# First-stage loads in one fixed order, and two blocks' sums of squares moved to GpSimd, in a hybrid Fourier/RWKV layer

## The chip, the cores and the metric

The kernel runs on one core of a Trainium2 chip. The metric is the device time in microseconds (us). Three runs of the kernel before took 1665.74, 1667.07 and 1669.72 us; the median is 1667.07. The profile comes from one more execution, whose own time is 1670.74 us and whose span, from the first to the last instruction, is 1668.9 us. Every time in the rows below is counted from the start of that span.

The engines are called as the profile calls them: PE (matrix), PEld (its weight loads), DVE (vector), ACT (scalar), POOL (GpSimd), SP (the queue that issues nearly all DMAs).

## The reference

One transformer-like layer over 1024 latent tokens of width 1024 and 256 context tokens. Only its first lines matter here:

```
mod_x = silu(c) @ ada_w + ada_b          # six vectors of 1024: shift, scale, gate, and again
mod_c = silu(c_ctx) @ ada_w + ada_b      # the same for the context
h  = rms_norm(x,   norm1_g) * (1 + scale) + shift
hc = rms_norm(ctx, norm1_g) * (1 + scale_c) + shift_c
u  = h @ w_in ;  uc = hc @ w_in[:, 512:] # the input projection
... Fourier mixing, RWKV scans, output projection, residual,
... second norm, gated feed-forward with a 3x3 grid convolution, final norm
```

All arithmetic is in 32 bits. For a product, a matrix is split into a high and a low part (`hi`, `lo`), and three products (hi·hi, lo·hi, hi·lo) are added up.

## The kernel before

The change lies in the first stage, `stage0`, and what follows it is the same program: input projection with the RWKV preparation beside it, Fourier part, scans, output projection, feed-forward. A scheduler arranges each engine's instructions in one fixed order, guided by its own model of their times; each engine then runs its own list strictly in order, and an instruction that has to wait holds up all behind it.

What stage 0 does:

- **Modulation.** `load_ad(q)` (L270) loads a 2 MB piece `ad` of `ada_w`, 512 of its 6144 columns. Pieces 0 and 1 give the shift for channels 0 to 511 and 512 to 1023, pieces 2 and 3 the scale. `ada_rows` (L276) multiplies a piece with the conditioning vector: 32 PE instructions, each recorded as two matmuls (x64 at L283), and ACT copies the result (`br`, L286). PE turns it (L292), and DVE adds the bias into `mod` (L321). Pieces 4 to 11 belong to later stages; the generator `ada_rest`, here `rest`, loads and multiplies them a little at a time. There are two buffers for pieces.
- **Positions.** x and ctx lie transposed, channels on partitions, in three blocks: two of 512 positions and the 256 of the context (`BLOCKS`). A block is eight tiles `x`, one for each k, that is each 128 channels.
- **`norm`** (L332) squares the eight tiles on ACT (L337), with two buffers `sq`, and adds the squares up on DVE (L339) into `sqs`. PE sums over the channels (L342); ACT and DVE form the reciprocal root `rs` (L264, L267); DVE writes four diagonal tiles `dg` (L348, two buffers), and PE spreads them over all partitions (`rsb`, L349).
- **`enter`** (L352) makes the two parts of h: for each k DVE forms v = x·G·rsb (L355, three buffers), ACT the high part hTh = v + shift (L357), DVE the low part hTl (L358). G comes from the scale (L368).
- **Products** (L385) of each block with two column tiles of `w_in` (m = 12 and 13) into `plat` and `pctx`. `weights` (L254) loads a tile (`wraw`, one buffer here), ACT writes its high part `whi` (L188), POOL its low part `wlo` (L189).

The first instruction after stage 0 that counts is the first product of the next column tile (L197), on PE.

**What sets the order of the loads.** All of them are issued by SP in the order of its list. A load waits until its buffer is free. It also waits until the load eight places before it has landed, since the program has eight semaphores for them.

Of the kernel before, what the change touches and what calls it, by code (L numbers as in the profile page):

```python
# [10 lines left out]
F32 = mybir.dt.float32  # L11
F32R = mybir.dt.float32r
# [151 lines left out]
class B:  # L164
# [105 lines left out]
    def load_ad(self, q):  # L270

        ad = self.wa.tile([128, 8, 512], F32, name="ad", bufs=2)
        self.nc.sync.dma_start(ad, self.a["ada"][:, :, q * 512:(q + 1) * 512])
        return ad
# [36 lines left out]
    def stage0(self, wk, hT, first, rest):  # L311
# [12 lines left out]
        def load_x(b, n):  # L324
            xs = []
            for k in range(8):
                x = wk.tile([128, 512], F32, name="x", bufs=16)[:, :n]
                nc.sync.dma_start(x, a["xT"][:, k, b:b + n])
                xs.append(x)
            return xs  # L330

        def norm(b, n, xs):  # L332
            who = int(b == T)
            acc = wk.tile([128, 512], F32, name="sqs", bufs=2)[:, :n]
            for k, x in enumerate(xs):
                sq = wk.tile([128, 512], F32, name="sq", bufs=2)[:, :n] if k else acc
                nc.scalar.activation(sq, x, AF.Square)  # L337
                if k:
                    nc.vector.tensor_add(acc, acc, sq)  # L339
# [12 lines left out]
        def enter(b, n, xs, rsb, who):  # L352
            for k, x in enumerate(xs):
# [6 lines left out]
        ads = [self.load_ad(2), self.load_ad(3)]  # L360
        self.adab = self.load("adab")
        self.n1g = self.load("n1g")
        self.n2g = self.load("n2g")
        xs = {0: load_x(*BLOCKS[0])}
        for q in (2, 3):
            modulation(q, ads.pop(0))
            ads.append(self.load_ad(q - 2))
        nc.vector.scalar_tensor_tensor(G, mod[:, 8:16, :], 1.0, self.n1g[:, :, None].to_broadcast([128, 8, 2]),  # L368
                                       op0=OP.add, op1=OP.mult)
        ws = [self.weights(self.wp, a["wi"][m], raws=1) for m in first]  # L370
        for n in (1, 2):
            xs[n] = load_x(*BLOCKS[n])
        stats = norm(*BLOCKS[0], xs[0])
        for q in (0, 1):
            modulation(q, ads[q])
        us = [(self.pl.tile([128, T], F32, name="plat", bufs=2), pp.tile([128, TC], F32, name="pctx", bufs=2)) for m in first]
        for n, (b, w) in enumerate(BLOCKS):
            if n:
                stats = norm(b, w, xs[n])
            enter(b, w, xs[n], *stats)  # L380
            for (wh, wl), (ul, uc) in zip(ws, us):
                o = uc if b == T else ul[:, b:b + w]
                for k in range(8):
                    for i, (wt, xt) in enumerate(((wh, hi), (wh, lo), (wl, hi))):
                        nc.tensor.matmul(o, wt[:, k, :], xt[:, k, b:b + w], start=k == 0 and i == 0, stop=k == 7 and i == 2)  # L385
            next(rest)
        return [[(ul, slice(0, T)), (uc, slice(T, TT))] for ul, uc in us]


    def stage1_open(self, wk):  # L390
        nc, a = self.nc, self.a
        const = self.const
        for n in ("cw", "w0", "a0", "kk_", "ka_", "rk_", "gng", "gnb", "bones", "bk", "mask"):
            setattr(self, n, self.load(n))
# [1136 lines left out]
```

## Time and profile before

| | |
|---|---|
| median of three runs | 1667.07 us (1665.74 to 1669.72) |
| profiled execution: time, span | 1670.74 us, 1668.9 us |
| busy: PE, DVE, ACT, POOL | 1506.0, 1120.0, 703.0, 510.6 us |
| granted PE clock, mean | 0.946 of full speed |
| stage 0, by its last product on PE | ends at 91.2 us |

How to read it: a busy share is an average over stages with different limits. For a change in one stage, the engine timelines of that stage say more: each row gives the start and the length of an instruction (or of neighbours of one kind), and in square brackets how long its engine had been idle before and what ended the wait. "PEclk" is the granted PE clock: 1.00 is 2.4 GHz and 0.50 is 1.2 GHz. DMA queue rows ("SPq") give the issue of a load, not its landing.

### The profile page before, as it was taken

Reading aid. Unit: us, or ns where it says so; the run is one execution under the profiler, and the core shown is the slowest. Engines: PE = TensorE matmul, PEld = TensorE weight load, DVE = VectorE, ACT = ScalarE, POOL = GpSimd, SP = SyncE. Lnnn points to the kernel's source line nnn. Section 1 sums busy time; section 2 is a strip of 40 time slices with the busy share of each in tenths; the row PEclk is TensorE's granted clock in tenths of the full one; section 3 lists DMA queues with packets and bytes.
Section 4 is the critical chain, followed back from the end, with each engine's and each line's share of the span. In section 5 each row is a group of like instructions: output and inputs, shape, how many; then the busy total and the mean of one; then the engine's idle time right before and its main releaser. Section 6 shows DMA issues by size and latency. Waiting matters only on the chain. (4 is left out here: it accounts for less than half of the span.)

```text
span 1668.9 us, 29107 instructions
## 1 busy us (share of the span) xinstructions
PE 1506.0 (90%) x11642; PEld 1217.8 (73%) x11642; DVE 1120.0 (67%) x1599; ACT 703.0 (42%) x1193; POOL 510.6 (31%) x443
## 2 busy tenths in 40 slices
PE   4899899898877689997988999999999998999996
PEld 3687676666656577786767888888888886786785
DVE  3614756666597786844556799999999998415513
ACT  3434656666443344426575322222222223445533
POOL 0013624443332342302132222222221222454454
PEclk7899999999977888999999999999999999999998
DMA  8676857787877687746310311111111116444542
GB/s 306 219 289 204 255 181 220 231 236 224 210 210 140 182 218 197 222 142 189 120 42 14 119 51 51 51 51 49 40 51 51 51 51 214 139 129 155 174 134 90
DMA packets 219319, 246.29 MB, mean 148 GB/s; under 512 B 63638, under 2 KB 173344, under 8 KB 219184
## 3 DMA queue, kind: packets, MB, share of 16 engines
q1 hardware_dynamic: 213008, 233.92, 46.1%
q0 software_dynamic: 6176, 10.51, 2.4%
q8 instruction: 92, 1.51, 0.4%
q14 instruction: 43, 0.35, 0.1%
HBM read 177.99 MB, written 66.33 MB: 146 GB/s over the span
## 5 line engine op out<-in xcount | busy, mean ns | idle before, releaser
L189 POOL TENSOR_TENSOR wlo<-wraw,whi 128x1024 fp32r<-128x1024 f32 x105 | 255.0, 2429 | 669.0 <-ACT whi L188 612.9
L1248 DVE SCALAR_TENSOR_TENSOR conv<-u,c_fcw,conv 128x945 f32<-128x945 f32 (+2 forms) x344 | 411.5, 1219 | 37.0 <-ACT conv L1241 29.1
L188 ACT ACTIVATE whi<-wraw 128x1024 fp32r<-128x1024 f32 x123 | 129.4, 1053 | 306.4 <-issue 173.7
L197 PE MATMUL u<-h2l,whi 128*128 128x512 f32 x672 | 207.0, 389 | 0.0
L197 PE MATMUL u<-h2h,whi 128*128 128x512 f32 x672 | 206.8, 389 | 0.0
L197 PE MATMUL u<-h2h,wlo 128*128 128x512 f32 x672 | 206.8, 389 | 0.0
L189 DVE TENSOR_TENSOR al<-act,ah 128x256 fp32r<-128x256 f32 (+1 forms) x88 | 62.8, 718 | 139.2 <-ACT ah L188 139.1
L197 PEld LDWEIGHTS u<-h2l,whi 128*128 128x128 f32 x672 | 126.1, 188 | 26.3
L197 PEld LDWEIGHTS u<-h2h,wlo 128*128 128x128 f32 x672 | 126.1, 188 | 26.2
L197 PEld LDWEIGHTS u<-h2h,whi 128*128 128x128 f32 x672 | 126.1, 188 | 26.0
L1305 PE MATMUL e<-wlo,ah 128*128 128x512 f32 x264 | 103.0, 390 | 2.9 <-POOL wlo L189 2.9
L1305 PE MATMUL e<-whi,al 128*128 128x512 f32 x264 | 103.0, 390 | 0.0
L188 ACT ACTIVATE ah<-act 128x256 fp32r<-128x256 f32 (+1 forms) x88 | 45.9, 523 | 134.8 <-PE e L1305 99.3
L197 PE MATMUL plat<-hTh,whi 128*128 128x512 f32 x272 | 97.1, 439 | 0.0
L197 PE MATMUL plat<-hTl,whi 128*128 128x512 f32 x272 | 90.4, 413 | 0.0
L197 PE MATMUL plat<-hTh,wlo 128*128 128x512 f32 x272 | 88.4, 404 | 0.4 <-DVE wlo L672 0.4
L1305 PE MATMUL e<-whi,ah 128*128 128x512 f32 x264 | 67.0, 389 | 0.0
L935 POOL COPY WV<-SV 64x512 f32<-64x512 f32 x40 | 27.7, 692 | 127.9 <-PE py L1001 33.7
L856 DVE TENSOR_TENSOR arrt<-arr 128x30 f32<-128x30 f32 (+9 forms) x150 | 53.4, 356 | 15.2 <-DMA arr<-xad 11.0
L197 PEld LDWEIGHTS plat<-hTl,whi 128*128 128x128 f32 x272 | 52.0, 194 | 14.0 <-issue 2.4
L197 PEld LDWEIGHTS plat<-hTh,wlo 128*128 128x128 f32 x272 | 52.3, 194 | 12.8 <-DVE wlo L672 0.8
L563 DVE TENSOR_TENSOR_SCAN cs<-c_rst,sg 128x256 f32<-128x256 f32 x40 | 33.2, 831 | 42.0 <-ACT sg L547 36.2
(290 smaller groups left out, 3090.0 us busy)
## 6 DMA issues: line engine op xcount, KB each, us to landing
wraw<-wd SPq DMA_DIRECT2D x66, 512.0 KB
ad<-ada SPq DMA_DIRECT2D x12, 2048.0 KB
wraw<-wu SPq DMA_DIRECT2D x42, 512.0 KB
xrd<-x SPq DMA_DIRECT2D x32, 640.0 KB
xs<-xrd SPq DMA_DIRECT2D x16, 1280.0 KB
xad<-x SPq DMA_DIRECT2D x80, 192.0 KB
xs<-xad SPq DMA_DIRECT2D x18, 512.0 KB
kvb<-kvd SPq DMA_DIRECT2D x16, 512.0 KB
```

Of the source, the lines that this page charges most:

```text
L188: self.nc.scalar.activation(hi, x, AF.Copy)
L189: (lo_eng or self.nc.gpsimd).tensor_sub(lo, x, hi.bitcast(F32))
L197: mm = self.nc.tensor.matmul(ps[:, b:b + n], wt[:, k, :], xt[:, k, b:b + n], start=k == 0 and i == 0, stop=k == 7 and i == 2)
L563: nc.vector.tensor_tensor_scan(cs, self.rst, o(sg), 0.0, op0=OP.mult, op1=OP.add)
L856: nc.vector.tensor_tensor(tv, arr[:, 0:j, j:j + 1].to_broadcast(sh), arr[:, j:j + 1, j + 1:].to_broadcast(sh), op=OP.mult)
L935: nc.gpsimd.tensor_copy(wv[r, h], sv[r, h])
L1248: nc.vector.scalar_tensor_tensor(og[:, R, Cc], ug[:, Ri, Ci], self.fcw[:, m, w:w + 1], og[:, R, Cc], op0=OP.mult, op1=OP.add)
L1305: nc.tensor.matmul(t, x[:, 128 * (i - i0):128 * (i - i0) + 128], w[:, j, 512 * (b - b0):512 * (b - b0) + 512], start=k == 0 and m == 0, st ...
```

## The change

1. The loads of stage 0 are chained: each is told to stand behind the one before on SP (`self.behind(self.link)`). The sequence is pieces 2 and 3 (scale), bias and first norm vector, the first block of x, first weights (m = 12), piece 0 (shift), second weights (m = 13), piece 1, the second and third block of x, and then `n2g`, the first of the later pieces, and the constants of the next stage.
2. The tiles `x` get 24 buffers, where they had 16.
3. In the second and third block the squares are added up on GpSimd (now L354).
4. Block 0 enters in two halves. Channels 0 to 3 need only piece 0; the products of tile m = 12 over them stand on PE ahead of the rows of piece 1, and the rest follows.

The diff, whole:

```diff
--- before.py
+++ after.py
@@ -270,7 +270,7 @@
     def load_ad(self, q):
 
         ad = self.wa.tile([128, 8, 512], F32, name="ad", bufs=2)
-        self.nc.sync.dma_start(ad, self.a["ada"][:, :, q * 512:(q + 1) * 512])
+        self.ad_load = self.nc.sync.dma_start(ad, self.a["ada"][:, :, q * 512:(q + 1) * 512])
         return ad
 
     def ada_rows(self, ad):
@@ -324,10 +324,25 @@
         def load_x(b, n):
             xs = []
             for k in range(8):
-                x = wk.tile([128, 512], F32, name="x", bufs=16)[:, :n]
-                nc.sync.dma_start(x, a["xT"][:, k, b:b + n])
+                x = wk.tile([128, 512], F32, name="x", bufs=24)[:, :n]
+                with self.behind(self.link):
+                    self.link = nc.sync.dma_start(x, a["xT"][:, k, b:b + n])
                 xs.append(x)
             return xs
+
+        def load_ad(q):
+            with self.behind(self.link):
+                ad = self.load_ad(q)
+            self.link = self.ad_load
+            return ad
+
+        def load_w(m):
+            raw = self.wp.tile([128, 8, 128], F32, name="wraw", bufs=1)
+            with self.behind(self.link):
+                self.link = nc.sync.dma_start(raw, a["wi"][m])
+            hi, lo = [self.wp.tile([128, 8, 128], F32R, name=x, bufs=2) for x in ("whi", "wlo")]
+            self.split(hi, lo, raw)
+            return hi, lo
 
         def norm(b, n, xs):
             who = int(b == T)
@@ -336,7 +351,7 @@
                 sq = wk.tile([128, 512], F32, name="sq", bufs=2)[:, :n] if k else acc
                 nc.scalar.activation(sq, x, AF.Square)
                 if k:
-                    nc.vector.tensor_add(acc, acc, sq)
+                    (nc.gpsimd if b else nc.vector).tensor_add(acc, acc, sq)
             st = pp.tile([128, 512], F32, name="aux")
             for i in range(n // 128):
                 nc.tensor.matmul(st[:, i:i + 1], acc[:, 128 * i:128 * i + 128], self.ones[:, 0:1], start=True, stop=True)
@@ -349,41 +364,59 @@
                 nc.tensor.matmul(rsb[:, 128 * i:128 * i + 128], self.ones, dg, start=True, stop=True)
             return rsb[:, :n], who
 
-        def enter(b, n, xs, rsb, who):
-            for k, x in enumerate(xs):
+        def enter(b, n, ks, rsb, who):
+            for k in ks:
+                x = xs[b][k]
                 v = wk.tile([128, 512], F32, name="v", bufs=3)[:, :n]
                 nc.vector.scalar_tensor_tensor(v, x, G[:, k, who:who + 1], rsb, op0=OP.mult, op1=OP.mult)
                 h, l = hi[:, k, b:b + n], lo[:, k, b:b + n]
                 nc.scalar.activation(h, v, AF.Identity, bias=mod[:, k, who:who + 1])
                 nc.vector.scalar_tensor_tensor(l, v, mod[:, k, who:who + 1], h.bitcast(F32), op0=OP.add, op1=OP.subtract)
 
-        ads = [self.load_ad(2), self.load_ad(3)]
+        def products(b, n, tiles, ks):
+            for m in tiles:
+                (wh, wl), (ul, uc) = ws[m], us[m]
+                o = uc if b == T else ul[:, b:b + n]
+                for k in ks:
+                    for i, (wt, xt) in enumerate(((wh, hi), (wh, lo), (wl, hi))):
+                        mm = nc.tensor.matmul(o, wt[:, k, :], xt[:, k, b:b + n], start=k == 0 and i == 0, stop=k == 7 and i == 2)
+            return mm
+
+        ads = {2: self.load_ad(2), 3: self.load_ad(3)}
         self.adab = self.load("adab")
         self.n1g = self.load("n1g")
-        self.n2g = self.load("n2g")
+        self.link = self.ad_load
         xs = {0: load_x(*BLOCKS[0])}
-        for q in (2, 3):
-            modulation(q, ads.pop(0))
-            ads.append(self.load_ad(q - 2))
+        ws = []
+        for q, m in zip((2, 3), first):
+            modulation(q, ads[q])
+            ws.append(load_w(m))
+            ads[q - 2] = load_ad(q - 2)
         nc.vector.scalar_tensor_tensor(G, mod[:, 8:16, :], 1.0, self.n1g[:, :, None].to_broadcast([128, 8, 2]),
                                        op0=OP.add, op1=OP.mult)
-        ws = [self.weights(self.wp, a["wi"][m], raws=1) for m in first]
-        for n in (1, 2):
-            xs[n] = load_x(*BLOCKS[n])
+        for b, n in BLOCKS[1:]:
+            xs[b] = load_x(b, n)
+        loads = self.loaded = self.link
+        with self.behind(loads):
+            self.n2g = self.load("n2g")
+        us = [(self.pl.tile([128, T], F32, name="plat", bufs=2), pp.tile([128, TC], F32, name="pctx", bufs=2)) for m in first]
         stats = norm(*BLOCKS[0], xs[0])
-        for q in (0, 1):
-            modulation(q, ads[q])
-        us = [(self.pl.tile([128, T], F32, name="plat", bufs=2), pp.tile([128, TC], F32, name="pctx", bufs=2)) for m in first]
-        for n, (b, w) in enumerate(BLOCKS):
-            if n:
-                stats = norm(b, w, xs[n])
-            enter(b, w, xs[n], *stats)
-            for (wh, wl), (ul, uc) in zip(ws, us):
-                o = uc if b == T else ul[:, b:b + w]
-                for k in range(8):
-                    for i, (wt, xt) in enumerate(((wh, hi), (wh, lo), (wl, hi))):
-                        nc.tensor.matmul(o, wt[:, k, :], xt[:, k, b:b + w], start=k == 0 and i == 0, stop=k == 7 and i == 2)
+        modulation(0, ads[0])
+        b, n = BLOCKS[0]
+        enter(b, n, range(4), *stats)
+        mm = products(b, n, (0,), range(4))
+        with self.behind(mm):
+            modulation(1, ads[1])
+        enter(b, n, range(4, 8), *stats)
+        products(b, n, (1,), range(4))
+        products(b, n, (0, 1), range(4, 8))
+        with self.behind(loads):
             next(rest)
+        for b, n in BLOCKS[1:]:
+            enter(b, n, range(8), *norm(b, n, xs[b]))
+            products(b, n, (0, 1), range(8))
+            next(rest)
+        self.link = None
         return [[(ul, slice(0, T)), (uc, slice(T, TT))] for ul, uc in us]
 
 
@@ -391,7 +424,8 @@
         nc, a = self.nc, self.a
         const = self.const
         for n in ("cw", "w0", "a0", "kk_", "ka_", "rk_", "gng", "gnb", "bones", "bk", "mask"):
-            setattr(self, n, self.load(n))
+            with self.behind(self.loaded):
+                setattr(self, n, self.load(n))
 
         for n in ("w0", "a0"):
             t = getattr(self, n)
```

The scheduler made new lists from this. Three places are shown, with names as in the code; line numbers above 340 have moved, so that L328 became L329, L337 L352, L339 L354, L342 L357, L349 L364, L357 L373, L385 L382, and the load of first weights L342.

SP, from the first tiles of x on, before:

```order
L328 DMA x<-xT 128x512 x8
L256 DMA wraw<-wi 128x1024
L328 DMA x<-xT 128x512 x8
L183 DMA c_cw<-cw 128x36
L183 DMA c_w_789<-w 128x8
L183 DMA c_a_791<-a 128x8
L273 DMA ad<-ada 128x8x512
L183 DMA c_kk__793<-kk_ 128x4
```

and now:

```order
L329 DMA x<-xT 128x512 x8
L342 DMA wraw<-wi 128x1024
L273 DMA ad<-ada 128x8x512
L342 DMA wraw<-wi 128x1024
L273 DMA ad<-ada 128x8x512
L329 DMA x<-xT 128x512 x8
L329 DMA x<-xT 128x256 x8
L183 DMA c_n2g<-n2g 128x8
L273 DMA ad<-ada 128x8x512
L183 DMA c_cw<-cw 128x36
```

Pieces 0 and 1 and the second weights now stand ahead of the second block of x, and the constants behind everything that stage 0 needs.

ACT, from the second block's squares to the last high part of block 0, before:

```order
L337 ACTIVATE sq<-x 128x512 x6
L286 ACTIVATE br<-aux 128x128
L357 ACTIVATE hTh<-v,mod 128x512 x3
L188 ACTIVATE whi<-wraw 128x1024
L337 ACTIVATE sqs<-x 128x256
L357 ACTIVATE hTh<-v,mod 128x512
L337 ACTIVATE sq<-x 128x256 x2
L286 ACTIVATE br<-aux 128x128
L337 ACTIVATE sq<-x 128x256 x3
L357 ACTIVATE hTh<-v,mod 128x512 x3
```

and now:

```order
L286 ACTIVATE br<-aux 128x128
L373 ACTIVATE hTh<-v,mod 128x512 x3
L352 ACTIVATE sqs<-x 128x512
L373 ACTIVATE hTh<-v,mod 128x512
L352 ACTIVATE sq<-x 128x512 x4
L352 ACTIVATE sqs<-x 128x256
L352 ACTIVATE sq<-x 128x512 x2
L286 ACTIVATE br<-aux 128x128
L352 ACTIVATE sq<-x 128x512
L373 ACTIVATE hTh<-v,mod 128x512 x3
L352 ACTIVATE sq<-x 128x256 x2
L373 ACTIVATE hTh<-v,mod 128x512
```

The first `br` in each is that of piece 0, the second that of piece 1. The squares of block 1 stood ahead of the first; seven of its eight, and one of block 2, now stand between the two.

PE, around the spreading of block 1's norm (the rows of `ad` in between are those of piece 4), before:

```order
L349 MATMUL aux<-dg,ones 128x128
L283 MATMUL aux<-ad,sc_93 32x128 x7
L349 MATMUL aux<-dg,ones 128x128
L283 MATMUL aux<-ad,sc_93 32x128 x13
L349 MATMUL aux<-dg,ones 128x128
L283 MATMUL aux<-ad,sc_93 32x128 x3
```

and now:

```order
L364 MATMUL aux<-dg,ones 128x128
L283 MATMUL aux<-ad,sc_93 32x128 x5
L364 MATMUL aux<-dg,ones 128x128
L283 MATMUL aux<-ad,sc_93 32x128 x13
L364 MATMUL aux<-dg,ones 128x128
L283 MATMUL aux<-ad,sc_93 32x128 x8
L364 MATMUL aux<-dg,ones 128x128
L283 MATMUL aux<-ad,sc_93 32x128 x6
```

Before, the first of the four spreads stands a few rows further up, with nine of the rows and four products behind it; the place on PE is otherwise the same.

## Rows read from the trace of the kernel before

**Rows 1.** Busy time by stretch: PE, PEld, DVE, ACT, POOL, clock, DMA share, GB/s.
```profile
0.00:92.00 92.00, 60.76 (x551) 48.78 (x555) 46.39 (x96) 38.56 (x67) 5.55 (x8) 0.85 0.68 239
92.00:200.00 108.00, 102.19 (x924) 77.46 (x917) 47.20 (x76) 48.85 (x104) 41.63 (x41) 0.99 0.84 270
...
460.00:700.00 240.00, 191.45 (x3060) 157.41 (x3060) 190.48 (x435) 99.41 (x211) 77.29 (x108) 0.82 0.76 193
```

**Rows 2.** PE timeline: start, length, instruction, idle before and what ended it.
```profile
24.81 1.84 PE L342 MATMUL aux<-ones,sqs 128*128 128x1 f32 x8 [2.06 <-DVE sqs L339]
...
31.12 1.22 PE L349 MATMUL aux<-dg,ones 128*128 128x128 f32 x4 [0.51 <-DVE dg L348]
35.58 3.64 PE L283 MATMUL aux<-ad,sc 128*32 128x128 f32 x64 [3.23 <-DMA ad<-ada]
...
62.67 0.38 PE L349 MATMUL aux<-dg,ones 128*128 128x128 f32 x2
...
67.08 0.49 PE L349 MATMUL aux<-dg,ones 128*128 128x128 f32 x2
...
92.80 0.73 PE L197 MATMUL plat<-hTh,whi 128*128 128x512 f32 x2
```

**Rows 3.** DVE timeline.
```profile
40.05 0.17 DVE L321 TENSOR_TENSOR mod<-aux,c_adab 128x8 f32<-128x8 f32 x1 [4.00 <-PE aux L292]
...
48.44 2.04 DVE L358 SCALAR_TENSOR_TENSOR hTl<-v,mod,hTh 128x512 fp32r<-128x512 f32 x1 [3.38 <-ACT hTh L357]
...
56.69 0.16 DVE L321 TENSOR_TENSOR mod<-aux,c_adab 128x8 f32<-128x8 f32 x1
...
59.63 0.74 DVE L358 SCALAR_TENSOR_TENSOR hTl<-v,mod,hTh 128x512 fp32r<-128x512 f32 x1
...
67.60 2.07 DVE L355 SCALAR_TENSOR_TENSOR v<-x,G,aux 128x512 f32<-128x512 f32 x3 [2.10 <-PE aux L349]
```

**Rows 4.** SP's queue: issues of loads.
```profile
26.89 0.55 SPq L273 DMA_DIRECT2D ad<-ada  x1
...
35.88 0.55 SPq L273 DMA_DIRECT2D ad<-ada  x1
...
51.50 8.57 SPq L328 DMA_DIRECT2D x<-xT  x2
```

**Rows 5.** Busy time and DMA rate while loads queue up; columns as in rows 1.
```profile
10.00:20.00 10.00, 7.67 (x129) 6.62 (x129) 1.91 (x4) 2.80 (x5) 0.00 (x0) 1.00 1.05 376
```

**Rows 6.** ACT timeline.
```profile
2.44 1.28 ACT L309 ACT_TABLE_LOAD   x1 [2.44 <-DMA c_cv<-cv]
...
24.16 1.06 ACT L188 ACTIVATE whi<-wraw 128x1024 fp32r<-128x1024 f32 x1 [0.42 <-DMA wraw<-wi]
...
27.57 0.26 ACT L264 ACTIVATE rs<-aux,eps 128x4 f32<-128x4 f32 x1
...
30.11 0.63 ACT L337 ACTIVATE sq<-x 128x512 f32<-128x512 f32 x1 [0.36 <-DVE sqs L339]
...
39.27 0.28 ACT L286 ACTIVATE br<-aux 128x128 f32<-128x128 f32 x1 [6.75 <-PE aux L283]
```

**Rows 7.** POOL timeline.
```profile
47.56 2.37 POOL L189 TENSOR_TENSOR wlo<-wraw,whi 128x1024 fp32r<-128x1024 f32 x1 [19.91 <-ACT whi L188]
```

**Rows 8.** Single lines: instructions, ns shortest/median/longest, first and last start.
```profile
L1332 POOL TENSOR_TENSOR x<-x,fgb x8: 1278/1642/1752, 1439.4 to 1655.2; 128x512 f32<-128x512 f32 x8
...
L583 POOL TENSOR_TENSOR bt<-kd x16: 729/905/1178, 166.2 to 475.8; 128x256 f32<-128x256 f32 x16
...
L1248 DVE SCALAR_TENSOR_TENSOR conv<-u,c_fcw,conv x344: 1189/1205/1271, 930.7 to 1409.0; 128x945 f32<-128x945 f32 x86, 128x1008 f32<-128x1008 f32 x43, 128x960 f32<-128x960 f32 x43
...
L189 DVE TENSOR_TENSOR wol<-wor,woh x8: 685/694/1770, 586.6 to 784.7; 128x512 fp32r<-128x512 f32 x8
```

**Rows 9.** Clock in short stretches; columns as in rows 1.
```profile
48.00:50.00 2.00, 2.00 (x19) 1.43 (x12) 1.56 (x1) 1.19 (x4) 1.93 (x1) 0.50 1.07 392
...
52.00:54.00 2.00, 2.00 (x11) 1.61 (x10) 0.00 (x0) 0.00 (x0) 0.00 (x0) 1.00 1.06 389
```

## The prediction

> **What bounds the kernel now.** I read the page first, then busy time by stretch, then the timelines of the first stage engine by engine. The stretches show where the change can act at all: in the first 92 us PE is busy for 60.8 us at a mean clock of 0.85, and from 92 to 200 us for 102.2 of 108 us at 0.99 [rows 1]. So the first stage is bound by waits of PE, and the stage behind it by PE itself. The border is the first product of the next column tile, at 92.80 us [rows 2]. What comes after waits for that point through PE's list, and no load behind it has a clock of its own, so I take a shift of this point as a shift of the end, one for one.
>
> Inside the first stage three moments pace everything. The shift for channels 0 to 511 is there at 40.05, that for 512 to 1023 at 56.69, and the first v of block 1 starts at 67.60 [rows 3]. From that v to 92.80 it is 25.2 us, in which DVE and PE run through blocks 1 and 2 with almost the same list before and after. Hence the gain is the number of us by which v of block 1 comes earlier. The two shifts are late because pieces 0 and 1 are issued at 26.89 and 35.88 [rows 4], behind sixteen tiles of x and most of the constants; PE starts on piece 0 at 35.58 having waited for the load [rows 2]. The last tiles of x are issued from 51.50 on, one of them held up for 8.57 us by its buffer [rows 4].
>
> **The change part by part.** All times are on the scale of the trace.
>
> *The loads.* Queued loads move 376 GB/s [rows 5]: a 2.1 MB piece takes 5.6 us, a 0.26 MB tile 0.7, 0.52 MB of weights 1.4. The first weights had landed by 24.16 [rows 6], and piece 0 is now right behind them: landed between 27.5 and 29.7. The second weights have one raw buffer with the first, so SP stands still until POOL has made `wlo` of the first: 24.16 + 1.06 for ACT [rows 6] + 2.37 for POOL [rows 7] is 27.7. This stop is new, and all later loads queue behind it. A load into an empty queue took from 0.76 to 2.44 here (the landing is in [rows 6]), so 1.7 us. The second weights land at 27.7 + 1.7 + 1.4 = 30.8, piece 1 at 36.5, the tiles of block 1 from 37.2 to 42, those of block 2 until 45, piece 4 at about 50.5, with the constants behind it. Removing `n2g` from the head, and the 24 buffers, save nothing by themselves.
>
> *First shift.* Block 0's norm loses the squares and sums of block 1 that stood in between. Its sum on PE ends at 26.65 [rows 2]; `rs`, which came at 27.57 after two foreign squares, comes at 26.8; the diagonals follow, and the four spreads take 0.6 us each at half clock [rows 2], until 30.1. The rows of piece 0 stand behind them on PE, so the landing no longer decides: 30.1 + 3.64 for the rows [rows 2] = 33.7. Before, the shift stood 0.8 us after the rows ended (39.22 to 40.05). Now 34.6, a gain of 5.5 us.
>
> *Second shift.* PE would have the rows of piece 1 at about 42 to 43.6. But ACT's copy `br` now stands behind six more squares of block 1 and one of block 2, and each square needs one of two buffers, which POOL's adds free. So POOL's pace enters here. No 128x512 add on POOL is in the trace of before; the nearest are a 128x512 multiplication, 1.28 us alone and up to 1.75, and a 128x256 add, 0.73 to 1.18 [rows 8]. I take 1.4 and 0.95, near the lower end, because for the first five adds DVE is nearly idle. The first square of block 1 ends at 37.8, the second, behind a high part of 0.7, at 39.1; the seven adds end at 40.6, 42.0, 43.4, 44.8, 46.2, 47.6 and 49.0. The seventh square waits for the fourth add: 44.8 + 0.6 [rows 6], then `br` 0.3 [rows 6] and 0.5 to the shift: 46.3. Gain 10.4 us. With 1.28 per add it is 45.8, with 1.75 it is 47.7.
>
> *Second half of block 0, and norm of block 1.* Its four low parts hTl on DVE take 0.74 us each [rows 3]. While POOL made the second `wlo`, from 47.56 to 49.93 [rows 7], one of them that started at 48.44 took 2.04 [rows 3]: it ended 0.55 after POOL did, so it stood still beside it. DVE's convolutions, which read one operand from PSUM, never took more than 1.27 in 344 runs [rows 8], with POOL's splits of weights beside many of them. So adds on POOL and low parts on DVE take turns. The first low part waits for the seventh add (49.0); then three adds of block 2 and four low parts alternate, 4 x 0.65 + 3 x 0.95 = 5.4, until 54.4; if DVE went first throughout it would be 51.6. I take 54. The reciprocal and the first diagonal stand behind them on DVE: 0.7 us, so the first spread is at 54.8. PE's 24 products of this half keep pace: 2 us hold some ten of them at full clock and half as many at 0.50 [rows 9], and even with half clock for the first half they end by 55.5. From the first spread to v it took 62.67 to 67.60, 4.9 us, 0.9 of them for four products that now stand elsewhere, so 4.0 at full clock, or up to 7 at half. Before, PE came to this place at 1.00; now it has had a pause from about 43.6 to 46.9, and in this stage the clock was still at 0.50 at 48 to 50 [rows 9]. I put 0.5 on top: v of block 1 at 59.3 instead of 67.6.
>
> *The sum.* 67.6 - 59.3 = 8.3 us. The profiled execution would come to 1670.7 - 8.3 = 1662.4; the median of the three runs lies 3.7 below the profiled execution, so 1667.1 - 8.3 = 1658.8 us.
>
> The adds taken from DVE (14, at about 0.6 and 0.3 us) give nothing beyond this: where they stood DVE was waiting for the shifts. The constants that DVE needs beside the diagonals land at about 51, under the low parts; were that cover gone, DVE would wait 1 to 2 us. Piece 4, whose rows stand between the spreads on PE, lands 4 us before they are reached.
>
> The Trainium skill has a rule that speaks against the fourth item ("SBUF — State Buffer", section "Who interferes with whom"): a DVE instruction with two SBUF inputs and a GpSimd instruction that reads SBUF cannot run together, and the one that comes second waits for the whole of the other. By that rule hTl, with both inputs in SBUF, waits, and v and the convolutions, with one in PSUM, don't; the trace agrees, with 2.04 us against 0.74 and 1.27 at most. Without the rule the sum would be 2.4 us better, v at 56.9.
>
> **The rivals.** *POOL stays out of the way* (A). The adds take 1.28, DVE goes first, the clock stays up. Then the second shift is at 45.8, the low parts end at 51, the products at 53, and v starts at 57; with the clock up early and squares that find their tiles sooner, 54. The gain is 10.6 to 13.6, and the time 1653.5 to 1656.5. For it: POOL is idle between its two splits [rows 7]. Against it: the 2.04.
>
> *POOL becomes the bound* (B), and the gain is spent. At 1.75 an add the seventh ends at 51.5, low parts and adds alternate until 58, and with the spreads at half clock v comes at 65.7. The gain is 1.9 us, the time 1665.2. For it: POOL's slow cases came exactly where DVE worked beside it [rows 8]. Against it: DVE has only four such low parts there, so most adds run alone.
>
> *The rest pays* (C). The scheduler's lists differ in a few places far behind stage 0 too, above all on DVE from 460 to 700 us, where it is busy for 190 of 240 us [rows 1] and where splits of output weights change places with the solver's steps. One such split took 0.69 to 1.77 us [rows 8]. Eight of them, each on the chain at its worst, are 14 us; from 8.3 us on they eat the gain, and at 14 the time is 1673, slower. For it: DVE is near full there. Against it: a swap of neighbours leaves the sum of work as it was, and most splits have slack.
>
> *The chain does not do what it says* (D): the order was never the limit, and DMA is. Then v would stay near 67 and the time at 1667. Against it: the very last tile of x is issued by 60.1 [rows 4] and belongs to block 2, so no load of block 1 can be what v waits for at 67.6.
>
> **How the numbers follow.** Forecast 0.66, A 0.16, B 0.10, C 0.05, D 0.03. The forecast's own range is 1655.5 to 1662 (v from 56 to 62.5). The range for 8 in 10 takes in most of A and most of B: 1654 to 1665. About 0.2%, 3.3 us, is what a measurement of this kernel can tell from no change. Faster by more: the forecast and A, with a fifth of B and C, 0.84. Within: most of B, D, some of C, 0.11. Slower: 0.05.
>
> **What would show it.** Right: shift rows on DVE near 34.6 and 46.3; POOL's seven 128x512 adds between 39 and 49; low parts of 1.3 to 2 us between 47 and 54; v of block 1 near 59; the first L197 product near 84.5. SP should stand still until about 27.7, with the DMA rate sagging at 28 to 29. Wrong: v at 59 but the end not earlier (C); the second shift above 48 (B); a low clock on PE from 46 through 60, which would cost more than the 0.5 put on top; or piece 4 landing after 55, so that PE's spreads wait for a load.

## The result, and the profile after

The changed kernel took 1657.8 us (median of 17 runs, 1651.09 to 1664.14); the kernel before, beside it, 1666.74 (17 runs, 1662.61 to 1672.26). The ratio is 0.9948, 95% interval [0.9934, 0.9962]: about 8.7 us less. The forecast was 1658.8. The profiled execution took 1663.68 us with a span of 1661.8, so it is one of the slower ones. Executions of one kernel differ by 13 us here and the moments of stage 0 by about 1, so what follows is read from the moments.

Busy time by stretch, against [rows 1]: PE, PEld, DVE, ACT, POOL, clock, DMA share, GB/s.

```profile
0.00:92.00 92.00, 66.72 (x660) 52.13 (x661) 39.77 (x83) 39.38 (x69) 23.55 (x22) 0.91 0.78 269
```

PE does 6 us more work in the first 92 us, at 0.91 of full clock instead of 0.85; POOL's 18 us more are the adds (16.0 us) and the work that now begins earlier.

SP's queue, against [rows 4]:

```profile
18.06 0.55 SPq L273 DMA_DIRECT2D ad<-ada  x1
27.23 0.33 SPq L342 DMA_DIRECT2D wraw<-wi  x1
27.65 0.55 SPq L273 DMA_DIRECT2D ad<-ada  x1
28.25 15.45 SPq L329 DMA_DIRECT2D x<-xT  x16
44.29 0.55 SPq L273 DMA_DIRECT2D ad<-ada  x1
```

Piece 0 goes out 8.8 us earlier than before, piece 1 8.2. Between them SP stands still until 27.23, when POOL has made the first low part of the weights; 27.7 was predicted.

ACT and POOL while block 1 is squared and added up (the number in square brackets is the wait, and what ended it). The two rows behind them are another view, POOL's adds: all fourteen, then the six that start before 48 us (ns shortest/median/longest, first and last start).

```profile
38.73 0.63 ACT L352 ACTIVATE sqs<-x 128x512 f32<-128x512 f32 x1 [2.98 <-DMA x<-xT]
...
41.94 0.63 ACT L352 ACTIVATE sq<-x 128x512 f32<-128x512 f32 x1 [0.93 <-POOL sqs L354]
...
46.00 0.63 ACT L352 ACTIVATE sq<-x 128x512 f32<-128x512 f32 x1 [0.71 <-POOL sqs L354]
46.54 0.26 ACT L286 ACTIVATE br<-aux 128x128 f32<-128x128 f32 x1
```

```profile
L354 POOL TENSOR_TENSOR sqs<-sqs,sq x14: 726/1252/1775, 40.6 to 56.7; 128x512 f32<-128x512 f32 x7, 128x256 f32<-128x256 f32 x7
L354 POOL TENSOR_TENSOR sqs<-sqs,sq x6: 1263/1272/1337, 40.6 to 47.4; 128x512 f32<-128x512 f32 x6
```

POOL's pace reaches ACT as predicted: a square waits for an add, and `br` of piece 1 stands behind those squares. The six adds of 128x512 before the low parts take 1.26 to 1.34 us, where 1.4 had been taken; the seventh, beside low parts, takes 1.77. The mean of the seven, 1.35, mixes the two.

DVE, against [rows 3]:

```profile
33.59 0.17 DVE L321 TENSOR_TENSOR mod<-aux,c_adab 128x8 f32<-128x8 f32 x1 [1.68 <-PE aux L292]
...
47.21 0.17 DVE L321 TENSOR_TENSOR mod<-aux,c_adab 128x8 f32<-128x8 f32 x1 [5.67 <-PE aux L292]
48.62 2.44 DVE L374 SCALAR_TENSOR_TENSOR hTl<-v,mod,hTh 128x512 fp32r<-128x512 f32 x2 [1.24 <-ACT hTh L373]
50.98 0.73 DVE L371 SCALAR_TENSOR_TENSOR v<-x,G,aux 128x512 f32<-128x512 f32 x1
51.64 1.88 DVE L374 SCALAR_TENSOR_TENSOR hTl<-v,mod,hTh 128x512 fp32r<-128x512 f32 x2
53.65 0.18 DVE L267 RECIPROCAL rs<-rs 128x4 f32<-128x4 f32 x1
...
60.73 2.07 DVE L371 SCALAR_TENSOR_TENSOR v<-x,G,aux 128x512 f32<-128x512 f32 x3 [2.11 <-PE aux L364]
```

The four low parts by themselves (ns shortest/median/longest):

```profile
L374 DVE SCALAR_TENSOR_TENSOR hTl<-v,mod,hTh x4: 739/880/1770, 48.6 to 52.5; 128x512 fp32r<-128x512 f32 x4
```

The shifts come 6.5 and 9.5 us earlier, v of block 1 6.9. Beside POOL's adds the low parts take 2.44 us for the first two and 1.88 for the others: one by one 0.75, 1.77, 0.74 and 1.01. The one of 1.77 ends 0.55 us behind the add that ran when it started. A v between them, with one operand in PSUM, keeps its 0.73.

PE, against [rows 2], and the clock in short stretches, against [rows 9] (columns as in the first fence):

```profile
48.64 0.80 PE L382 MATMUL plat<-hTh,whi 128*128 128x512 f32 x2 [1.47 <-ACT hTh L373]
...
52.16 1.16 PE L357 MATMUL aux<-ones,sqs 128*128 128x1 f32 x8
...
56.94 0.38 PE L364 MATMUL aux<-dg,ones 128*128 128x128 f32 x2
57.25 0.62 PE L283 MATMUL aux<-ad,sc 128*32 128x128 f32 x10
...
63.02 0.58 PE L357 MATMUL aux<-ones,sqs 128*128 128x1 f32 x4
...
84.34 0.73 PE L197 MATMUL plat<-hTh,whi 128*128 128x512 f32 x2
```

```profile
48.00:50.00 2.00, 1.36 (x3) 0.80 (x4) 1.38 (x2) 2.00 (x4) 1.92 (x2) 0.79 1.05 401
50.00:52.00 2.00, 2.00 (x6) 1.59 (x5) 2.00 (x3) 0.78 (x3) 1.92 (x3) 0.50 1.04 341
52.00:54.00 2.00, 2.00 (x13) 1.77 (x13) 1.71 (x4) 1.39 (x4) 1.92 (x2) 0.85 0.20 23
...
70.00:74.00 4.00, 4.00 (x28) 2.55 (x27) 3.87 (x8) 2.62 (x5) 0.00 (x0) 1.00 0.15 54
```

From 48.64 to 56.94 PE is never idle: 24 products of block 0, the third to the eighth at half clock, and block 1's sums between them. The first two diagonals follow the reciprocal on DVE at once (53.65); the first spread stands behind the products. The first L197 product is at 84.34, 8.5 us earlier.

Single lines far behind (instructions, ns shortest/median/longest, first and last start), against [rows 8]:

```profile
L1282 DVE SCALAR_TENSOR_TENSOR conv<-u,c_fcw,conv x344: 1189/1204/1270, 923.5 to 1401.4; 128x945 f32<-128x945 f32 x86, 128x1008 f32<-128x1008 f32 x43, 128x960 f32<-128x960 f32 x43
...
L1366 POOL TENSOR_TENSOR x<-x,fgb x8: 1272/1642/1755, 1431.7 to 1648.1; 128x512 f32<-128x512 f32 x8
```

They start 7.2 and 7.7 us earlier: most of the 8.5 arrives at the end.

### The profile page after: what moved, and what is told of

Read it like the earlier page. It is cut to its first block, busy times and chain, and to the rows that moved or that the text cites. A ratio compares the mean times of both kernels' runs of the same rounds, so it can differ in the third digit from the quotient of the medians.

```text
span 1661.8 us, 29106 instructions
## 1 busy us (share of the span) xinstructions
PE 1499.5 (90%) x11642; PEld 1210.6 (73%) x11642; DVE 1117.2 (67%) x1585; ACT 702.7 (42%) x1193; POOL 525.8 (32%) x457
## 3 DMA queue, kind: packets, MB, share of 16 engines
q1 hardware_dynamic: 213008, 233.92, 46.3%
## 5 line engine op out<-in xcount | busy, mean ns | idle before, releaser
L197 PE MATMUL u<-h2h,wlo 128*128 128x512 f32 x672 | 207.0, 389 | 0.0
L197 PE MATMUL u<-h2h,whi 128*128 128x512 f32 x672 | 206.9, 389 | 0.0
L197 PE MATMUL u<-h2l,whi 128*128 128x512 f32 x672 | 206.9, 389 | 0.0
L197 PEld LDWEIGHTS u<-h2h,wlo 128*128 128x128 f32 x672 | 126.1, 188 | 26.2
L197 PEld LDWEIGHTS u<-h2l,whi 128*128 128x128 f32 x672 | 126.1, 188 | 26.2
L197 PEld LDWEIGHTS u<-h2h,whi 128*128 128x128 f32 x672 | 126.1, 188 | 26.1
L197 PE MATMUL plat<-hTh,whi 128*128 128x512 f32 x272 | 98.5, 445 | 0.0
L197 PE MATMUL plat<-hTl,whi 128*128 128x512 f32 x272 | 90.4, 414 | 0.0
L197 PE MATMUL plat<-hTh,wlo 128*128 128x512 f32 x272 | 89.0, 407 | 0.4 <-DVE wlo L706 0.4
L969 POOL COPY WV<-SV 64x512 f32<-64x512 f32 x40 | 27.6, 692 | 129.3 <-PE py L1035 41.4
L197 PEld LDWEIGHTS plat<-hTl,whi 128*128 128x128 f32 x272 | 52.9, 197 | 14.0 <-issue 2.1
L197 PEld LDWEIGHTS plat<-hTh,wlo 128*128 128x128 f32 x272 | 52.6, 196 | 13.2 <-DVE wlo L706 0.9
```

The lines of the kernel that those rows point to most:

```text
L197: mm = self.nc.tensor.matmul(ps[:, b:b + n], wt[:, k, :], xt[:, k, b:b + n], start=k == 0 and i == 0, stop=k == 7 and i == 2)
L969: nc.gpsimd.tensor_copy(wv[r, h], sv[r, h])
```

## The experiments

All moments are from one profiled execution each, in us. Experiments 1 to 4 ran on one chip, 5 to 8 on another, 9 to 12 on a third, each group beside the kernel before. The last column sets the gain at the first L197 product (92.80 less the moment) beside the gain in the total (one less the ratio, times 1667 us).

| kernel | adds of blocks 1, 2 | shifts | v of block 1 | first L197 | ratio, 95% interval | gain at L197, by the ratio |
|---|---|---|---|---|---|---|
| before | DVE | 40.05, 56.69 | 67.60 | 92.80 | 1 |  |
| changed | POOL | 33.59, 47.21 | 60.73 | 84.34 | 0.9948 [0.9934, 0.9962] | 8.5, 8.7 |
| 1 changed, adds on DVE | DVE | 33.06, 46.74 | 59.18 | 82.62 | 0.9981 [0.9962, 1.0000] | 10.2, 3.2 |
| 2 before, adds on POOL | POOL | 41.79, 55.43 | 68.10 | 93.30 | 1.0006 [0.9981, 1.0032] | -0.5, -1.0 |
| 3 changed, 16 buffers x | POOL | 33.64, 47.66 | 58.75 | 94.98 | 1.0009 [0.9989, 1.0029] | -2.2, -1.5 |
| 4 changed, no halves | POOL | 33.24, 42.98 | 59.92 | 83.53 | 0.9950 [0.9932, 0.9968] | 9.3, 8.3 |
| 5 as 4, own raw buffer | POOL | 33.84, 44.69 | 59.80 | 85.00 | 0.9948 [0.9927, 0.9968] | 7.8, 8.7 |
| 6 loads only | DVE | 33.85, 47.20 | 60.06 | 85.09 | 0.9985 [0.9969, 1.0002] | 7.7, 2.5 |
| 7 before, 24 buffers x | DVE | 40.25, 54.13 | 66.46 | 91.49 | 1.0028 [1.0009, 1.0047] | 1.3, -4.7 |
| 8 changed, again | POOL | 33.46, 46.57 | 61.81 | 85.43 | 0.9948 [0.9929, 0.9968] | 7.4, 8.7 |
| 9 loads only, lists of before | DVE | 33.98, 47.44 | 61.21 | 86.41 | 0.9964 [0.9943, 0.9985] | 6.4, 6.0 |
| 10 loads only, again | DVE | 34.07, 46.84 | 60.77 | 85.80 | 0.9972 [0.9950, 0.9993] | 7.0, 4.7 |
| 11 as 6, 3 buffers sq | DVE | 33.38, 47.30 | 59.95 | 84.99 | 0.9955 [0.9937, 0.9973] | 7.8, 7.5 |
| 12 as 4, 4 buffers sq | POOL | 33.89, 48.85 | 62.81 | 88.00 | 0.9932 [0.9911, 0.9954] | 4.8, 11.3 |

**1. The adds back on DVE.**

```diff
-                    (nc.gpsimd if b else nc.vector).tensor_add(acc, acc, sq)
+                    nc.vector.tensor_add(acc, acc, sq)
```

> The changed kernel with the squares of all blocks added up on DVE again; loads, 24 buffers and halves as changed. Theory (the order of the loads is the gain, and POOL's adds give a part of it back, through the squares' two buffers and by taking turns with the low parts): second shift at 45 to 46 instead of 47.2, no low part of block 0 over 0.8 us, first v of block 1 at 56 to 58 instead of 60.7, first L197 product at 80 to 82 instead of 84.3, time 2 to 4 us under the changed kernel. Rival (DVE needed the relief): 14 adds, some 7 us, stand between the low parts again, v of block 1 at 62 to 64, L197 at 86 to 88, time 2 to 4 us over the changed kernel.

The rows of DVE:

```profile
48.08 1.41 DVE L374 SCALAR_TENSOR_TENSOR hTl<-v,mod,hTh 128x512 fp32r<-128x512 f32 x2
...
54.65 0.17 DVE L432 TENSOR_SCALAR c_w<-c_w 128x8 f32<-128x8 f32 x1 [1.71 <-DMA c_w<-w]
...
59.18 2.06 DVE L371 SCALAR_TENSOR_TENSOR v<-x,G,aux 128x512 f32<-128x512 f32 x3 [2.12 <-PE aux L364]
```

The low parts went back to their old length, so POOL's adds had lengthened them: low parts and adds do take turns. But v came only 1.55 us earlier, and the total did not follow: 1662.09 us, some 4 more than the changed kernel. So the theory missed the time. The rival's time came, but not its mechanism, since v and the L197 product (82.62) are earlier, not later.

**2. The kernel before with the adds on POOL.** The line of experiment 1, the other way round.

> The kernel before with one thing changed: the squares of the second and third block are added up on POOL. Theory: DVE waits for the shifts there, so nothing is gained; v of block 1 within 1.5 us of 67.6, L197 within 1.5 of 92.8, time within 2 us of before. Rival (the adds on POOL are a gain of their own): v at 62 to 65, time 3 to 5 us under before.

No gain: stage 0 ends 0.5 us later, the total is the same. Moving the adds is worth nothing measurable while the loads keep their old sequence.

**3. The changed kernel with 16 buffers for x.**

```diff
-                x = wk.tile([128, 512], F32, name="x", bufs=24)[:, :n]
+                x = wk.tile([128, 512], F32, name="x", bufs=16)[:, :n]
```

> The changed kernel with 16 buffers for tiles of x. Theory (the buffers matter little): block 2's tiles wait for v of block 0, so its last tile and piece 4 come some 6 us later, but block 1 does not: v of block 1 at 59 to 62, L197 at 84 to 87, time 0 to 2 us over the changed kernel. Rival (the early third block is a large part of the gain): L197 at 88 or later, time 4 us or more over it.

A miss, and the clearest result: the whole gain is gone, as the rival had it, although both shifts come within 0.5 us of the changed kernel's and v of block 1 comes 2 us earlier. SP's queue, then PE, then DVE:

```profile
52.19 0.33 SPq L329 DMA_DIRECT2D x<-xT  x1
...
53.09 1.26 SPq L273 DMA_DIRECT2D ad<-ada  x2
```

```profile
61.94 1.18 PE L283 MATMUL aux<-ad,sc 128*32 128x128 f32 x32 [0.89 <-DMA ad<-ada]
...
78.08 0.51 PE L357 MATMUL aux<-ones,sqs 128*128 128x1 f32 x4
79.56 0.50 PE L364 MATMUL aux<-dg,ones 128*128 128x128 f32 x2 [0.97 <-DVE dg L363]
79.99 1.92 PE L283 MATMUL aux<-ad,sc 128*32 128x128 f32 x26
81.84 0.80 PE L364 MATMUL aux<-dg,ones 128*128 128x128 f32 x2
```

```profile
68.90 0.17 DVE L432 TENSOR_SCALAR c_w<-c_w 128x8 f32<-128x8 f32 x1 [0.81 <-DMA c_w<-w]
...
82.67 1.26 DVE L371 SCALAR_TENSOR_TENSOR v<-x,G,aux 128x256 f32<-128x256 f32 x3 [3.06 <-PE aux L364]
```

The last tile of x waits 8.0 us for its buffer and goes out at 52.19, and with the fixed sequence everything behind it is late too: piece 4 is issued at 53.09 instead of 44.29, and the constants follow it. But the waits for these loads are short, 0.89 us on PE at 61.94 and 0.81 on DVE at 68.90. PE's list, which the scheduler made anew for 16 buffers, is different too. Block 2's sums, at 63.02 in the changed kernel, now stand behind all products of block 1 and all rows of piece 4, at 78.08, though POOL's last add had ended at 57.9. Rows of piece 5 stand between block 2's spreads, and those of piece 6 ahead of the first L197 product, one piece more than in the changed kernel. v of block 2 starts at 82.67, 11.3 us later than in the changed kernel. How much of this is the wait itself and how much the list was not separated.

**4. Block 0 in one piece.**

```diff
-        modulation(0, ads[0])
+        for q in (0, 1):
+            modulation(q, ads[q])
         b, n = BLOCKS[0]
-        enter(b, n, range(4), *stats)
-        mm = products(b, n, (0,), range(4))
-        with self.behind(mm):
-            modulation(1, ads[1])
-        enter(b, n, range(4, 8), *stats)
-        products(b, n, (1,), range(4))
-        products(b, n, (0, 1), range(4, 8))
+        enter(b, n, range(8), *stats)
+        products(b, n, (0, 1), range(8))
```

> The changed kernel with block 0 entered in one piece: both shifts first, then all eight channels' high and low parts, then the products. Theory (halves matter little, since PE has time before the second shift): second shift at 44 to 46.5, v of block 1 at 58 to 62, L197 within 1.5 us of 84.3, time within 2 us of the changed kernel. Rival (the early products are a large part): products of block 0 end 3 us later or more, v of block 1 after 63, time 3 us or more over it.

The halves are worth nothing measurable: 1656.38 us. The second shift is 4.2 us earlier, v only 0.8. DVE and ACT show why:

```profile
42.98 0.17 DVE L321 TENSOR_TENSOR mod<-aux,c_adab 128x8 f32<-128x8 f32 x1 [2.16 <-PE aux L292]
46.56 2.44 DVE L374 SCALAR_TENSOR_TENSOR hTl<-v,mod,hTh 128x512 fp32r<-128x512 f32 x2 [3.42 <-ACT hTh L373]
```

```profile
45.29 0.63 ACT L352 ACTIVATE sq<-x 128x512 f32<-128x512 f32 x1 [0.25 <-POOL sqs L354]
45.83 1.93 ACT L373 ACTIVATE hTh<-v,mod 128x512 fp32r<-128x512 f32 x3
```

The shift is there at 42.98, but the high parts stand on ACT behind squares that wait for POOL.

**5. No stop of SP for the second weights.** Experiment 4 with

```diff
-            raw = self.wp.tile([128, 8, 128], F32, name="wraw", bufs=1)
+            raw = (self.wp if m == 12 else wk).tile([128, 8, 128], F32, name="wraw", bufs=1)
```

> Block 0 in one piece, as in the run without halves, and the second weights' raw tile in a buffer of its own, so that SP need not wait for POOL's first low part. PE's, ACT's and POOL's lists are those of the run without halves; on SP only the issues of constants behind the loads of stage 0 change places, on DVE four small operations. Theory (the stop is covered, since the second shift comes at 42.98 from the squares' queue and v of block 1 from POOL's seventh add, not from a load): SP goes on at about 19 instead of 27.2, piece 1 lands some 3 to 4 us earlier, block 1's tiles too; the squares begin only behind block 0's high parts, so the second shift moves by at most 2 us, the seventh add by 0 to 1.5, v of block 1 is at 58.5 to 60 (59.92 with the stop), the first L197 product at 82 to 83.6, and the total within 0.2% of the run without halves, 1655 to 1658. Rival (the new stop of SP is on the path: every load behind it is late by 8 us and POOL's adds wait for tiles): v at 56 or earlier, L197 at 80 or earlier, the total 1652 to 1654.

SP issues the second weights at 18.53 instead of 27.13 and piece 1 at 20.10, and nothing follows: v at 59.80 against 59.92, 1656.09 us. The L197 product at 85.00 lies above the expected 83.6. That is the clock, not the loads: the same two microseconds of PE in this run and in experiment 4 (columns as in the first fence):

```profile
64.00:66.00 2.00, 2.00 (x6) 1.59 (x5) 2.00 (x5) 1.34 (x3) 0.00 (x0) 0.50 1.04 392
64.00:66.00 2.00, 2.00 (x10) 1.64 (x9) 2.00 (x6) 1.28 (x2) 0.00 (x0) 1.00 1.02 387
```

The stop costs nothing measurable.

**6. The loads alone.** Experiments 1 and 4 together: the fixed sequence and 24 buffers, nothing else.

> Only the sequence of the loads and the 24 buffers: block 0 in one piece, all adds on DVE. Theory (the sequence with its buffers is the whole gain; halves nothing, adds on POOL a loss in stage 0): shifts at 33 and 41 to 43, low parts of 0.75 each, v of block 1 at 57 to 59, the first L197 product at 81 to 83, 10 us before the old 92.80. With that passed one for one the total is 1655 to 1658; as the lists far behind differ as in the run with the adds on DVE, which ended at 1662, it may come to 1662 again, and then what stands behind stage 0 has taken 4 us back. Rival (the adds on POOL are needed, since DVE has too much to do there): v at 61 or later, L197 at 85 or later, total 1660 or more with stage 0 as the place of the loss.

Stage 0 gives nearly the whole gain, 7.7 us at the first L197 product, so the sequence with its buffers is what moved the stage. v is later than expected, by PE: the diagonals are ready at 53, and the first spread stands until 56.04 behind block 0's products, as in the changed kernel. But the total, 1662.37, keeps less than half of it.

**7. 24 buffers without the sequence.** The edit of experiment 3, the other way round, in the kernel before.

> The kernel before with 24 buffers for x and nothing else; the scheduler puts three tiles of block 2 ahead of piece 0 and the other five right behind it, and piece 1 behind most constants. Theory (it is the sequence, pieces 0 and 1 ahead of block 1, that pays; buffers alone leave both pieces late): first shift at 39 to 42 (before 40.05), second at 50 to 55 (before 56.69), v of block 1 at 62 to 67 (before 67.60), the first L197 product at 88 to 92.5, a gain of 0 to 4 us, 1662 to 1667. Rival (the wait for the buffers was the limit, and the sequence only a way to order them): v at 60 to 61 and L197 at 84 to 85 as in the changed kernel, 1656 to 1659.

The first shift stays, the second comes 2.6 us earlier, stage 0 gains 1.3 us, and the total is 0.28% longer; what costs it behind stage 0 was not located. Buffers without the sequence are no gain.

**8. The changed kernel again**, with no edit.

> The changed kernel itself, unaltered, beside the other runs on the same chip, so that they can be set against it and not only against the kernel before. Expected 1655 to 1660, ratio 0.993 to 0.996; in its profile the shifts at 33.6 and 47.2, v of block 1 at 60.7 and the first L197 product at 84.3, each within 0.3 us if these places repeat from run to run.

1658.14 us and the same ratio; the shifts repeat within 0.7, v and L197 within 1.1 us, wider than the 0.3 expected.

**9 and 10. Do other lists eat what the loads-only kernel lacks?** Experiment 9 is experiment 6 with four buffers `sq` instead of two, which brings back the lists of before behind stage 0; 10 is experiment 6 unaltered.

> The sequence of the loads and the 24 buffers alone, all adds on DVE, block 0 in one piece, as in the run with the loads only; four buffers for the squares where there were two. With that the scheduler's lists of all engines behind the first stage come out as in the kernel before (DVE, ACT and SP each with one neighbour's swap near the end), while the run with the loads only had other lists at two places, among the pairs (about 180 to 460 us) and among the solver's steps (460 to 700). Theory (what the loads-only run lost, some 4 us behind stage 0, is the price of its other lists): stage 0 as there or better, since ACT's squares wait less, v of block 1 at 56 to 60, the first L197 product at 80.5 to 85, and the total follows one for one: 1655 to 1658, ratio 0.993 to 0.996. Rival (adds on DVE cost something behind the first stage by themselves, or the total of 1662 is the run's scatter): 1661 to 1663 again.

> The run with the loads only, unaltered, beside the one with the lists of before, on the same chip. Theory: 1661 to 1663 again, the first L197 product at 84 to 85.5, so 4 us above what stage 0 gives. Rival (scatter): 1656 to 1659, as its stage 0 would have it.

In both executions of the loads-only kernel the solver's last multiplication (line 886 there, line 890 in the changed kernel) starts 216.9 and 216.4 us after the last masking among the pairs (line 670, 674); in 9 it is 207.2, in the changed kernel 207.2. The rows of 10, then of 9:

```profile
L886 DVE TENSOR_TENSOR arrt<-arr x150: 185/352/2047, 447.2 to 703.7; 128x30 f32<-128x30 f32 x10, 128x58 f32<-128x58 f32 x10, 128x84 f32<-128x84 f32 x10, 128x108 f32<-128x108 f32 x10
L670 DVE TENSOR_TENSOR x<-aux,c_mask x80: 400/678/693, 158.5 to 487.3; 128x512 f32<-128x512 f32 x64, 128x256 f32<-128x256 f32 x16
```

```profile
L886 DVE TENSOR_TENSOR arrt<-arr x150: 180/351/1314, 445.1 to 692.9; 128x30 f32<-128x30 f32 x10, 128x58 f32<-128x58 f32 x10, 128x84 f32<-128x84 f32 x10, 128x108 f32<-128x108 f32 x10
L670 DVE TENSOR_TENSOR x<-aux,c_mask x80: 407/676/692, 157.0 to 485.7; 128x512 f32<-128x512 f32 x64, 128x256 f32<-128x256 f32 x16
```

So the loads-only kernel lost some 9 us at that place in both executions. The lists alone don't make it: in experiment 1, with the same lists there, it was 210.3, and in the other eleven traces it lies between 205.2 and 209.8.

In the total 9 missed its expected 1655 to 1658 with 1662.37, 10 came to 1663.32, just above its own range, and their intervals overlap. But 9 missed in stage 0 first: its L197 product came at 86.41 where 80.5 to 85 was expected, with the clock at about half from 64 to 68. Behind stage 0 nothing is missing. Its lists there are those of the kernel before but for a swap or two, its first L197 product is 6.4 us earlier, and its ratio is worth 6.0 us. Of all runs it is the cleanest test of the loads by themselves, and its interval does not hold 1.

**11 and 12. DVE against POOL with the same lists behind stage 0.** 11 is experiment 6 with three buffers `sq`, 12 is experiment 4 with four.

> Loads in the new sequence, 24 buffers, block 0 in one piece, three buffers for the squares, all adds on DVE. Behind the first stage its lists are those of the next run, which has the adds of blocks 1 and 2 on POOL; so the two differ in stage 0 alone. Theory (low parts and POOL's adds take turns, so in stage 0 the adds are better off on DVE): low parts of 0.75 each, v of block 1 at 57 to 59.5, the first L197 product 1 to 3 us ahead of the next run's, the total 1 to 3 us less than the next run's. Rival (POOL's adds relieve DVE): v and the total 1 us or more later than the next run's.

> As the run before it, but the adds of blocks 1 and 2 on POOL, with four buffers for the squares, so that ACT's squares wait less for POOL. Theory: second shift at 41 to 44, the low parts up to 2.4 us beside POOL's adds, v of block 1 at 59 to 61.5, the first L197 product at 83 to 85.5, the total 1655 to 1659 and 1 to 3 us above the run with the adds on DVE. Rival: 1 us or more below it.

In stage 0 the sign is as expected, L197 at 84.99 against 88.00, but it decides nothing: 12 missed all its own moments (its shift at 48.85 where 41 to 44 was expected), because in this one execution PE got piece 1, and ACT the first tile of block 1, late:

```profile
41.30 2.71 PE L283 MATMUL aux<-ad,sc 128*32 128x128 f32 x64 [3.99 <-DMA ad<-ada]
```

```profile
41.84 0.63 ACT L352 ACTIVATE sqs<-x 128x512 f32<-128x512 f32 x1 [5.80 <-DMA x<-xT]
```

In the total the sign is the other way, 1659.75 against 1657.1 us, with intervals that overlap. No kernel here is measurably better than the changed one; 12 has the lowest ratio, but its interval holds 0.9948.

**What stays open.** The five results with the new sequence, 24 buffers and the adds on POOL (changed, 4, 5, 8, 12) have ratios of 0.9932 to 0.9950, the five with the adds on DVE (1, 6, 9, 10, 11) 0.9955 to 0.9985, while their first L197 products lie at 85.3 and 85.0 on average. The last column of the table tells more. The three kernels that keep far less than they gained in stage 0 are 1, 6 and 10, and these three have the same lists of DVE, ACT and POOL behind stage 0, which no other kernel here has. 9 and 11 have their adds on DVE too, but other lists, and keep nearly all of it. So the loss goes with those lists, not with adds on DVE as such. It is clear of the noise in 1 and 6 alone, the chips are mixed, and what in the lists costs it is located only in part (the solver's steps in 6 and 10). For 12 the stage 0 of the traced execution says little, since its loads were late. Not tested: the changed kernel with its buffers and adds on POOL, but without the sequence.

## Why the prediction was right

**The sum.** v to L197, the step said, is 25.2 us before and after; 8.3 us would pass one for one. It measured 8.5 at L197 and 7.1 at the end of these two executions, 8.9 between the medians. The mechanism is the one predicted, but several terms were off and cancelled: that the sum came within 0.2 us at L197 is luck.

- *First shift*: 34.6 predicted, 33.59 measured. As argued, PE took the rows of piece 0 right behind the spreads, not behind the load.
- *Second shift*: 46.3 predicted, 47.21 measured. The squares' two buffers and `br` behind them were as described. The adds ahead of `br` took 1.26 to 1.34 us, which gave back 0.4; the first tile of block 1 came 1.5 us later than the 37.2 I had.
- *Low parts and adds take turns*: until 54 predicted, 53.5 measured. Two of the four low parts took 1.77 and 1.01 us beside the adds, where all four took 0.73 to 0.75 in experiment 1. The Trainium skill ("SBUF — State Buffer", section "Who interferes with whom") states that a DVE instruction with two SBUF inputs contends with a GpSimd instruction that reads SBUF; the trace agrees with these numbers. It speaks against the third item of the change, the adds, not the fourth, as the prediction has it.
- *First spread*: 54.8 predicted, 56.94 measured. This term was mis-sized. I had let PE's 24 products keep pace with the low parts; they did not, since they began late (48.64), ran six at half clock, and had block 1's sums (1.16 us) among them. So PE, not the turns, held the spread, and without the turns (experiment 1) v gained 1.55 us, not the 2.4 I gave the rule.
- *v of block 1*: 59.3 predicted, 60.73 measured, for the same reason. From the first spread to v it took 3.8 us at full clock; the 0.5 put on top for a low clock was not needed here.
- *v to L197*: 25.2 predicted, 23.6 measured. The clock's rows of before show what went (columns as in the first fence):

```profile
68.00:70.00 2.00, 1.17 (x5) 0.64 (x5) 2.00 (x5) 1.86 (x4) 0.00 (x0) 1.00 0.39 35
70.00:72.00 2.00, 1.95 (x8) 1.59 (x8) 2.00 (x4) 0.94 (x3) 0.00 (x0) 0.64 0.90 345
72.00:74.00 2.00, 2.00 (x7) 1.54 (x6) 2.00 (x6) 1.34 (x3) 0.00 (x0) 0.51 1.04 396
```

  There PE had waited for v's high parts at 68 to 70 and then ran at about half clock for most of 4 us; now it was at 1.00 through this part. That gave back what the spread had cost. The other traces show the same two values: 23.4 to 23.6 us where the clock stays at 1.00 in this stretch (changed, 1, 4, 8), and 25.0 to 25.2 in the nine where it falls to about half for some 3 us (3, with its other list, is apart). The prediction had no term for this.

**What the prediction had wrong.** "Removing `n2g` from the head, and the 24 buffers, save nothing by themselves" is true of the buffers as it stands (experiment 7: no gain), and it missed that the sequence cannot do without them: with 16 the whole 8.9 us are lost. The stalled x tiles were in the rows of before [rows 4]; the row of 8.57 us holds a wait of 7.3 for a buffer. Once all loads are chained, that stall is everyone's, and the scheduler's lists change with it. The adds taken from DVE were priced at nothing: in stage 0 that held, and in the total no run shows otherwise except 1, 6 and 10, with their lists. A slip without weight: 24.16 + 1.06 + 2.37 is 27.6, not 27.7.

**The rivals.** A (POOL out of the way) had the length of the adds right (1.28, measured 1.26 to 1.34 until DVE worked beside them), but fell with the rest: turns were taken and the clock went down. B (POOL the bound) fell too: only one add took 1.77, and PE held the spread. D fell with experiment 6. C, the rest pays, is not true of the changed kernel, whose first L197 product and end move together; it is true of 1 and of the loads-only kernel, where some 5 us of the gain went missing behind stage 0. The wait of 1 to 2 us for the constants, had the low parts not covered it, came in experiment 1: 1.71 us.

## What to carry to other kernels

Where one engine issues all loads, put what the first dependent step needs ahead of what only the second needs, and count the buffers of the tiles that now stand in front: a tile that waits for its buffer holds back every load behind it, and a scheduler may rearrange the lists around that. Of several edits made together, take each one back alone; here the halves and SP's stop were worth nothing measurable, and one buffer count was worth all. Effects of a few us on a program of 1660 need moments in the trace, since a rescheduled list far away can move the total by as much. To test one edit by itself, look for a variant that leaves the lists elsewhere as they were, as experiment 9 did.

## What the runs showed of the hardware

- An add of 128x512 on POOL took 1.26 to 1.34 us, the same add on DVE, for block 0, 0.69. Where an add and a low part met, each stood still for the other: 1.77 us for the seventh add instead of 1.27, and 1.77 for the low part behind it instead of 0.75.
- After PE's pause from 44.3 to 48.6 us, broken by one 0.33 us instruction, its granted clock was 1.00 until 48, 0.79 from 48 to 50 and 0.50 from 50 to 52, when it was busy throughout; it was back at 1.00 from 54. It fell behind the pause, not in it.
- The same stretch from v of block 1 to the first L197 product took 23.6 us with the clock at 1.00 (changed) and 25.2 where it was 0.64 and 0.51 for 4 us (before).
- The same loads in the same order arrive at different times: ACT got the first tile of block 1 at 38.01 (experiment 4), 38.73 (changed), 39.32 (11) and 41.84 (12), though piece 1, the load ahead of it, was issued within 0.7 us of the same moment in all four.
